# A decoder trunk on eight cores: convolution taps that read PSUM, SiLU on ScalarE, casts off GpSimd, and an instruction order planned with the contention of VectorE and GpSimd and with slack for TensorE

## The chip, the cores and the metric

The kernel runs on the 8 cores of one Trainium2 chip, each core with one prompt sequence of 2048 tokens and 16 sample sequences of 4 tokens. The metric is device time in microseconds (us) of the slowest core. These kernels have a second, slower state in some executions: the records of some cores show a lower TensorE clock than those of the others. Only fast runs are compared here.

Names: PE is TensorE (matmuls), PEld its weight loads, DVE is VectorE, ACT is ScalarE, POOL is GpSimd, SP is SyncE.

## The reference, cut to what matters

```python
def trunk_layer(x, c, h0, buf_a, buf_b, ...):          # four layers of this; cut
    shift, scale, gate = split(silu(c) @ w_c + b_c, 3)
    h = layer_norm(x) * (1 + scale) + shift
    a_x, a_z, b_cg, b_bg, b_x, b_z, g_a, g_b = split(h @ w_in)       # 8 x 1024 columns
    xa, new_buf_a = causal_conv(a_x, buf_a, conv_a_w)                # 4 taps
    xa = xa + conv_a_b
    hs, h_last = rglru(xa, ...)          # two block-diagonal gates of xa, exp, sqrt, a scan
    o_a = (hs * silu(a_z)) @ w_a_out
    yb, new_buf_b = causal_conv(b_cg * b_x, buf_b, conv_b_w)         # 3 taps
    o_b = (b_bg * yb * silu(b_z)) @ w_b_out
    out = (sigmoid(g_a) * o_a + sigmoid(g_b) * o_b) @ w_o
    res = ALPHA * x + gate * out
    return layer_norm(res) * ln_g + ln_b, ...
```

## The kernel before

Channels lie on the 128 partitions, tokens on the free axis. The 2112 tokens of a core are three jobs of W = 704, and a slot is one job in one layer. A projection for 128 channels of a job is 16 matmuls of 352 columns into a "pair", a PSUM tensor that the program declares as 128x1024 fp32, with 352 columns in use in each half of 512. The program has four pairs. A pair can be filled again only when every reader of its block is through.

The order of every engine's instructions is computed when the kernel is built. Operations are recorded with what they read and write, a modelled cost, and an engine. A greedy planner then simulates the five queues, takes for each engine the earliest candidate in a window, and assigns PSUM pairs. Its order is what runs; on the chip, semaphores enforce the dependencies. The loop of the planner in the kernel before:

```python
        while left:
            best = None
            for e in ENGS:
                lst = pend[e]
                if not lst:
                    continue
                window = PE_WINDOW if e == "pe" else EW_WINDOW
                cands = []
                for i, op in enumerate(lst[:window]):
                    rdy = 0.0
                    for d in op.deps:
                        if d.finish is None:
                            break
                        t = d.finish if d.eng == e and d.dma is None else d.finish + SYNC
                        if t > rdy:
                            rdy = t
                    else:
                        pr = None
                        if op.blk is not None and op.blk.pair is None:
                            pt = None
                            for k, users in enumerate(pairs):
                                t = 0.0
                                for u in users:
                                    if u.finish is None:
                                        break
                                    t = max(t, u.finish + SYNC)
                                else:
                                    if pt is None or t < pt:
                                        pt, pr = t, k
                            if pr is None:
                                continue
                            rdy = max(rdy, pt)
                        sw = e == "act" and op.tbl != 0 and op.tbl & cur_tbl == 0
                        st = max(rdy, free[e])
                        cands.append((st + (TBL_COST if sw else 0.0), i, op, sw, pr, st))
                if not cands:
                    continue
                first = min(c[0] for c in cands)
                c = min((c for c in cands if c[0] <= first + QUANT), key=lambda c: c[1])
                if best is None or c[0] < best[1][0]:
                    best = (e, c)
            assert best is not None, "no operation can be scheduled"
            e, (st, i, op, sw, pr, _) = best
            if e == "act" and op.tbl:
                cur_tbl = op.tbl if sw or cur_tbl == 0 else op.tbl & cur_tbl
            if pr is not None:
                have = set(map(id, op.deps))
                op.deps += [u for u in pairs[pr] if id(u) not in have]
                op.blk.pair = pr
                pairs[pr] = op.blk.users
            free[e] = st + op.cost
            if op.dma is not None:
                dma_free = max(dma_free, st + 1.0) + op.nbytes / DMA_RATE
                op.finish = dma_free + 1.2
            else:
                op.finish = st + op.cost + op.lat
            del pend[e][i]
            newq[e].append(op)
            left -= 1
        self.q = newq
        return max(free.values())
```

The modelled costs: a DVE operation of n columns is `0.1 + n * 1.04 / 1000` us (0.83 for 704), with 0.06 more for a scalar read per partition; a POOL operation is `0.2 + n * 0.0021` (1.68 for 704).

The operations that the change touches, for one chunk of 128 channels (c) of a slot. `act` goes to ACT, `tt` to the engine named, `stt` to DVE, `T(s)` is a slot of the SBUF tile TMP, `ps(blk)` the PSUM block:

```python
            def f_ax(c=c, x=x):
                x["u0"] = U.get()
                blk = Blk()
                proj(x["u0"], 0, blk)
                a = take("p1")
                r = x["xa"] = take("p1")
                pB = PSTB[l][c][1]
                cp("pool", T(a, 0, 3), PST[:, l, c, 1:4], [pB], [TMPB[a]])
                act(halves(T(r)), ps(blk), AF.Identity, [blk, PRMB], [TMPB[r]], bias=prm(l, c, 4), scale=prm(l, c, 3),
                    psum=True)
                act(halves(T(a, 3, 3 + W)), ps(blk), AF.Copy, [blk], [TMPB[a]], psum=True)
                cp("pool", PST[:, l, c, 1:4], T(a, npr, npr + 3), [TMPB[a]], [pB])
                if smp:
                    sv = v3(AXS[:, :], 7)
                    st = v3(SST[:, c, 16:64], 3)
                    cp("pool", sv[:, :, 0:3], st, [SSTB[c]], [AXSB], n=48)
                    cp("pool", sv[:, :, 3:7], v3(T(a, 3 + npr, 3 + W), ST), [TMPB[a]], [AXSB], n=64)
                    cp("pool", st, sv[:, :, 4:7], [AXSB], [SSTB[c]], n=48)
                for kk in (2, 1, 0):
                    stt(T(r, 0, npr), T(a, kk, kk + npr), prm(l, c, kk), T(r, 0, npr), ALU.mult, ALU.add,
                        [TMPB[a], PRMB, TMPB[r]], [TMPB[r]], n=npr)
                if smp:
                    xv = v3(T(r, npr, W), ST)
                    for kk in (2, 1, 0):
                        stt(xv, sv[:, :, kk:kk + ST], prm(l, c, kk), xv, ALU.mult, ALU.add,
                            [AXSB, PRMB, TMPB[r]], [TMPB[r]], n=NSMP)
                give("p1", a)
                b = x["xab"] = (k * NCH + c) % 2
                cp("pool", XAb[:, b, :], T(r), [TMPB[r]], [XAbB[b]], n=W)

            def f_az(c=c, x=x):
                blk = Blk()
                proj(x["u0"], 1, blk)
                U.release(x["u0"])
                z = x["tz"] = take("p1")
                act(halves(T(z)), ps(blk), AF.Tanh, [blk], [TMPB[z]], scale=0.5, psum=True)
                stt(halves(T(z)), halves(T(z)), 1.0, ps(blk), ALU.add, ALU.mult, [TMPB[z], blk], [TMPB[z]])
```

SiLU of a_z (and, alike, of b_z) is (tanh(z/2) + 1) * z: an ACT operation and a DVE operation that both read the pair. The short convolution and the gates, cut before their sample-token parts:

```python
            def f_cg(c=c, x=x):
                blk = Blk()
                proj(x["u1"], 0, blk)
                U.release(x["u1"])
                b = x["cb"]
                tt("dve", halves(T(b, 2, 2 + W)), ps(blk), halves(T(b, 2, 2 + W)), ALU.mult, [blk, TMPB[b]], [TMPB[b]])
                cp("pool", PST[:, l, c, 4:6], T(b, npr, npr + 2), [TMPB[b]], [PSTB[l][c][2]])
                y = x["yb"] = take("p1")
                act(T(y), T(b, 2, 2 + W), AF.Identity, [TMPB[b], PRMB], [TMPB[y]], scale=prm(l, c, 10))
                for kk in (1, 0):
                    stt(T(y, 0, npr), T(b, kk, kk + npr), prm(l, c, 8 + kk), T(y, 0, npr), ALU.mult, ALU.add,
                        [TMPB[b], PRMB, TMPB[y]], [TMPB[y]], n=npr)
            ...
            def f_gate(c=c, x=x):
                b, xa = x["xab"], x["xa"]
                br, bi = Blk(), Blk()
                for o, blk in ((0, br), (1, bi)):
                    mm(blk, [(wcol(WG, c, o), lambda t, b=b: XAb[:, b, t * HW:(t + 1) * HW])], [WGB, XAbB[b]])
                r, i, m = take("p1"), take("p1"), take("p1")
                act(halves(T(r)), ps(br), AF.Tanh, [br, DERB], [TMPB[r]], bias=HB[:, 0, l, c:c + 1], scale=0.5, psum=True)
                act(halves(T(i)), ps(bi), AF.Tanh, [bi, DERB], [TMPB[i]], bias=HB[:, 1, l, c:c + 1], scale=0.5, psum=True)
                s = SH[:, l, c:c + 1]
                act(T(r), T(r), AF.Exp, [TMPB[r], DERB], [TMPB[r]], bias=s, scale=s)
                act(T(m), T(r), AF.Square, [TMPB[r]], [TMPB[m]])
                stt(T(i), T(i), 1.0, T(xa), ALU.add, ALU.mult, [TMPB[i], TMPB[xa]], [TMPB[i]])
                act(T(m), T(m), AF.Sqrt, [TMPB[m]], [TMPB[m]], bias=0.25, scale=-0.25)
                tt("pool", T(i), T(i), T(m), ALU.mult, [TMPB[i], TMPB[m]], [TMPB[i]])
                hB = PSTB[l][c][0]
                ...
```

## Time and profile before

| kernel before | value |
|---|---|
| time, median of 3 runs | 2960.91 us (2958.0 to 2961.5) |
| undisturbed core 5 of the profiled run: span, clock | 2955.3 us, 0.976 |
| PE / DVE / ACT / POOL busy on core 5 | 2690 / 2236 / 1648 / 1490 us |
| PE waits on core 5, all together | 242 us |

The profiled execution: cores 2 and 3 took 3005.5 and 3005.9 us at a clock of 0.952, the other six 2953 to 2956 us at 0.975 to 0.977. Every reading below is therefore of core 5, which is undisturbed.

From core 5's page, the busy line (time, share of the span, instructions) and the chain that ended last, by engine and then by line of the kernel:

```profile
PE 2690.3 (91%) x18144; PEld 1735.5 (59%) x18144; DVE 2235.9 (76%) x2521; ACT 1648.1 (56%) x1967; POOL 1490.3 (50%) x1818
...
PE 68%; DVE 14%; issue 10%; ACT 5%; POOL 1%; DMA 1%; DVEq 0%; SPq 0%; ACTq 0%; POOLq 0%
PE PS L398 67%; DVE TMP L378 6%; DVE TMP L374 6%; ACT TMP L365 4%; DMA X<-x 1%; ACT L365 1%; DVE X L378 1%; DVE TMP L579 1%; POOL TMP L374 1%; ACT X L365 1%; PE PS L773 0%; DVEq L209 0%; DVE X L374 0%; DVE MG L374 0%; ACT HN L365 0%
```

PE is busy for 91% of the span and makes up 68% of the chain. The other 32% of the chain is work of other engines that PE waited for, and time in which an engine waited for nothing that the profile shows (issue).

Busy times by stretch of the span, same core. The columns after the length are busy time and count of instructions by engine, then the granted clock, the DMA share and GB/s:

```profile
core 5: us, PE busy (x) PEld busy (x) DVE busy (x) ACT busy (x) POOL busy (x), PEclk, DMA share, GB/s
0.00:215.00 215.00, 124.08 (x947) 78.14 (x948) 150.20 (x161) 114.36 (x144) 109.13 (x124) 0.94 0.85 153
215.00:2600.00 2385.00, 2252.47 (x15155) 1455.57 (x15154) 1850.54 (x2056) 1376.86 (x1638) 1239.82 (x1501) 0.98 0.76 131
```

The first 215 us are the start-up. After that, between 215 and 2600 us, PE is idle for 2385 - 2252.5 = 132.5 us. In stretches without a stall, 136 to 137 matmuls start in 20 us, 146.5 ns each.

What PE waited for on that core (the releaser; us in total, times, longest):

```profile
engine line waited for: us in total, times, longest us
PE PS L398 <- DVE TMP L378: 91.7, 56, 3.6
PE PS L398 <- DVE LNR L374: 47.4, 5, 31.0
PE PS L398 <- ACT TMP L365: 40.3, 26, 5.0
PE PS L398 <- DVE TMP L374: 15.1, 19, 1.5
```

The four largest are shown; the whole list adds up to 242 us. The largest releaser is the DVE scalar_tensor_tensor on TMP. SiLU and the merge end with such an operation as the last reader of their block, so a pair stays taken until DVE gets to it. The wait for LNR is mostly the start (31.0 us at once).

Groups of instructions kept apart by shape, core 5 (busy us, mean ns of one; then idle time before them and what ended it):

```profile
L378 DVE SCALAR_TENSOR_TENSOR TMP<-TMP,PRM 128x704 f32<-128x704 f32 x320 | 368.2, 1151 | 133.4 <-ACT TMP L365 111.7 <-DVE TMP L378 1.8
L378 DVE SCALAR_TENSOR_TENSOR TMP<-TMP,PS 128x704 f32<-128x704 f32 x384 | 335.1, 879 | 130.4 <-PE PS L398 102.7 <-ACT TMP L365 26.2
...
L365 ACT ACT_TABLE_LOAD x227 | 291.2, 1283 | 49.6 <-PE PS L398 44.8 <-DVE TMP L378 1.3
...
L374 DVE TENSOR_TENSOR TMP<-X,TMP 128x704 f32<-128x704 f32 x192 | 208.3, 1089 | 11.1 <-ACT TMP L365 7.9 <-ACT HN L365 1.4 <-ACT X L365 0.7
...
L378 DVE SCALAR_TENSOR_TENSOR X<-PS,MOD,X 128x704 f32<-128x704 f32 x64 | 60.3, 943 | 28.5 <-PE PS L398 28.5
```

The first group holds convolution taps (two SBUF inputs), the second SiLU and the merge (one PSUM input). They have the same shape and the same operation, but take 1.151 and 0.879 us. The timeline shows where the difference comes from (x2 is two operations shown as one; of the taps, the window that was asked for cuts off a third):

```profile
start us, us, engine line op out<-in xcount [idle before <-releaser]
...
1416.26 1.68 POOL L374 TENSOR_TENSOR YB<-TMP 128x704 bf16<-128x704 f32 x1 [4.08 <-DVE TMP L374]
...
1416.82 4.14 DVE L374 TENSOR_TENSOR TMP<-X,TMP 128x704 f32<-128x704 f32 x2
1417.89 2.32 POOL L374 TENSOR_TENSOR TMP<-TMP 128x704 f32<-128x704 f32 x1
...
1422.83 3.50 DVE L378 SCALAR_TENSOR_TENSOR TMP<-TMP,PRM 128x704 f32<-128x704 f32 x2
...
1423.90 1.68 POOL L374 TENSOR_TENSOR YA<-TMP 128x704 bf16<-128x704 f32 x1
```

Two DVE operations (x2) that need about 0.9 us each take 4.14 us beside two POOL multiplies, and of the two taps (3.50 us together) the one beside another multiply takes 2.46 us; one of the three POOL multiplies takes 2.32 us, the others 1.68.

Sorted one by one in core 5's trace, the 184 taps of 704 columns that had no POOL operation beside them (DMA issues not counted) took 0.950 us in the mean and at most 0.954; the 105 that had one beside them for over half of their time took 1.559 us. SiLU and merge, with their PSUM input, took 0.883 us without POOL and 0.875 beside it. So a tap from SBUF is slower only where POOL runs.

### The profile page before, as it was taken

How to read it: one execution, taken by the hardware profiler on the slowest of the kernel's cores; microseconds unless marked ns; L12 is line 12 of the kernel's file. 1: busy time of each engine (PE TensorE's matmuls, PEld its weight loads, DVE VectorE, ACT ScalarE, POOL GpSimd, SP SyncE). 2: the span in 40 equal slices, each digit the busy share in tenths (PEclk: the TensorE clock that was granted, in tenths of full speed). 3: DMA queues.
4: the chain of work that ended last, by engine and by line, in shares of the span. 5: the costliest groups of instructions: out<-in, count | busy, mean ns of one | idle time of the engine just before them, and what ended most of it. 6: DMA issues, size and time to landing. Idle time of an engine off the chain costs nothing.

```text
span 3005.9 us, 54078 instructions; the slowest of 8 cores (2953.4 to 3005.9 us)
## 1 busy us (share of the span) xinstructions
PE 2753.6 (92%) x18144; PEld 1758.7 (59%) x18144; DVE 2243.5 (75%) x2521; ACT 1648.4 (55%) x1967; POOL 1487.4 (49%) x1818
## 2 busy tenths in 40 slices
PE   1789998999999999999999999899999899999996
PEld 1456665665565666565565566566556566566553
DVE  3886678778668778878877877877866787776745
ACT  3665556546546556555564655654645655653532
POOL 3574356455336436546535535655543653644611
PEclk9899999998899999999999999999889999999977
DMA  9878987877787887786897797777767578687671
GB/s 189 150 115 126 148 119 123 147 106 143 116 135 107 154 154 107 134 146 100 149 157 116 140 156 122 138 131 109 137 98 134 88 132 152 103 170 117 94 164 50
DMA packets 116479, 389.03 MB, mean 129 GB/s; under 512 B 12912, under 2 KB 13168, under 8 KB 116208
## 3 DMA queue, kind: packets, MB, share of 16 engines
q0 software_dynamic: 83520, 304.12, 67.2%
q1 hardware_dynamic: 32688, 81.45, 8.7%
q8 instruction: 151, 2.47, 0.3%
q14 instruction: 120, 0.98, 0.1%
HBM read 653.33 MB, written 36.27 MB: 229 GB/s over the span
## 4 chain that ended last, share of the span: by engine, by line
PE 72%; DVE 12%; issue 8%; ACT 5%; POOL 1%; DMA 1%; DVEq 0%; SPq 0%; ACTq 0%; POOLq 0%
PE PS L398 72%; DVE TMP L378 5%; DVE TMP L374 5%; ACT TMP L365 3%; DMA X<-x 1%; ACT L365 1%; DVE X L378 1%; POOL TMP L374 1%; DVE TMP L579 1%; ACT X L365 0%; PE PS L773 0%; DVEq L209 0%; POOL PST L389 0%; ACT HN L365 0%; POOL SST L389 0%
## 5 line engine op out<-in xcount | busy, mean ns | idle before, releaser
L398 PE MATMUL PS<-HN,WB 128*128 128x352 bf16 x12288 | 1983.6, 322 | 131.3 <-DVE TMP L378 73.0
L398 PEld LDWEIGHTS PS<-HN,WB 128*128 128x128 bf16 x12288 | 1224.4, 100 | 833.9 <-issue 156.8
L365 ACT ACTIVATE TMP<-PS 128x704 f32<-128x704 f32 x624 | 461.0, 752 | 420.0 <-PE PS L398 381.4
L378 DVE SCALAR_TENSOR_TENSOR TMP<-TMP,PRM 128x704 f32<-128x704 f32 (+1 forms) x480 | 524.7, 1093 | 184.1 <-ACT TMP L365 151.4
L404 POOL DMA_DIRECT2D WB<-wmain x528 | 295.4, 560 | 619.8 <-PE PS L398 506.3
L374 POOL TENSOR_TENSOR TMP<-TMP 128x704 f32<-128x704 f32 x240 | 435.0, 1814 | 166.1 <-ACT TMP L365 157.5
L378 DVE SCALAR_TENSOR_TENSOR TMP<-TMP,PS 128x704 f32<-128x704 f32 x384 | 335.2, 880 | 158.9 <-PE PS L398 123.0
L365 ACT ACTIVATE TMP<-X 128x704 f32<-128x704 f32 x192 | 149.5, 788 | 335.4 <-DVE X L378 146.3
L365 ACT ACT_TABLE_LOAD x227 | 291.2, 1283 | 56.3 <-PE PS L398 51.7
L389 POOL COPY PST<-TMP 128x1 f32<-128x1 f32 (+2 forms) x288 | 146.6, 509 | 285.5 <-ACT TMP L365 146.7
L398 PE MATMUL PS<-YB,WB 128*128 128x352 bf16 x1536 | 255.0, 321 | 8.5 <-DVE TMP L378 8.5
L398 PE MATMUL PS<-YA,WB 128*128 128x352 bf16 x1536 | 255.0, 321 | 0.1
L374 POOL TENSOR_TENSOR YB<-TMP 128x704 bf16<-128x704 f32 x96 | 180.2, 1878 | 143.1 <-DVE TMP L374 139.1
L398 PE MATMUL PS<-MG,WB 128*128 128x352 bf16 x1536 | 245.4, 317 | 5.0 <-DVE TMP L378 2.8
L374 DVE TENSOR_TENSOR TMP<-PS,TMP 128x704 f32<-128x704 f32 x192 | 170.1, 886 | 97.2 <-PE PS L398 93.4
L374 DVE TENSOR_TENSOR TMP<-X,TMP 128x704 f32<-128x704 f32 x192 | 208.7, 1091 | 14.3 <-ACT TMP L365 11.1
L365 ACT ACTIVATE TMP<-TMP,PRM 128x704 f32<-128x704 f32 x96 | 84.6, 881 | 240.6 <-DVE TMP L374 238.2
L398 PEld LDWEIGHTS PS<-YB,WB 128*128 128x128 bf16 x1536 | 152.9, 100 | 94.8 <-issue 10.6
L374 DVE TENSOR_TENSOR TMP<-TMP 128x704 f32<-128x704 f32 x192 | 181.5, 950 | 31.4 <-ACT TMP L365 21.3
L398 PEld LDWEIGHTS PS<-MG,WB 128*128 128x128 bf16 x1536 | 151.8, 99 | 88.4 <-issue 6.7
L398 PEld LDWEIGHTS PS<-YA,WB 128*128 128x128 bf16 x1536 | 153.2, 100 | 85.4 <-issue 0.8
L365 ACT ACTIVATE TMP<-TMP 128x704 f32<-128x704 f32 (+1 forms) x241 | 190.1, 789 | 20.9 <-DVE TMP L579 3.6
(56 smaller groups left out, 2100.8 us busy)
## 6 DMA issues: line engine op xcount, KB each, us to landing
WB<-wmain POOLq DMA_DIRECT2D x528, 512.0 KB, 7.5
xres<-X SPq DMA_DIRECT2D x72, 352.0 KB, 11.1
X<-xres SPq DMA_DIRECT2D x72, 352.0 KB, 8.5
WB<-wc POOLq DMA_DIRECT2D x48, 512.0 KB, 8.7
X<-x SPq DMA_DIRECT2D x48, 352.0 KB, 9.8
y<-X SPq DMA_DIRECT2D x24, 352.0 KB, 5.9
WG<-wmain POOLq DMA_DIRECT2D x4, 512.0 KB, 7.2
SST<-sst SPq DMA_DIRECT2D x4, 384.0 KB, 7.8
```

The lines of the kernel that those rows point to most:

```text
L365: return P.add("act", lambda e: e.activation(out=res(out), in_=res(in_), func=func, **kw), reads, writes, cost=0.14 + 0.09 * nap + n * 0.0 ...
L374: return P.add(eng, lambda e: e.tensor_tensor(out=res(out), in0=res(in0), in1=res(in1), op=op), reads, writes, cost=cost, lat=0.05)
L378: return P.add("dve", lambda e: e.scalar_tensor_tensor(out=res(out), in0=res(in0), scalar=scalar, in1=res(in1), op0=op0, op1=op1), reads, ...
L389: return P.add(eng, lambda e: e.tensor_copy(out=res(out), in_=res(in_)), reads, writes, cost=(0.19 + n * 0.0009) if eng == "pool" else dco ...
L398: ins = e.matmul(PS[blk.pair][:, t * 512:t * 512 + HW], w, mov(t), start=(i == 0), stop=(i == len(steps) - 1))
L404: return P.add(eng, lambda e: e.dma_start(out=out, in_=src), reads, writes, dma=tag, cost=0.56 if eng == "pool" else 0.08, nbytes=nbytes)
L579: P.add("dve", lambda e: e.tensor_tensor_scan(out=T(m), data0=T(r), data1=T(i), initial=PST[:, l, c, 0:1], op0=ALU.mult, op1=ALU.add), [TM ...
```

## The change

Its intent: give DVE less to do and less contention, free PSUM sooner, and make the planned order hold on the chip. The parts:

1. Matmul outputs of a pair become contiguous (the first 352 columns move to the end of the first half of 512), so that one access of 704 columns runs over both halves, with 160 free columns in front. Taps read the pair itself, at an offset; the 2 or 3 columns of history are copied in front of it.
2. SiLU is one ACT operation.
3. Casts and history copies move from POOL to ACT.
4. The planner plans POOL's operations and those of DVE without a PSUM operand one after another, as if they shared one thing (the field `port`; "the port" below is this part of the plan, a model of the stretch from 0.950 to 1.559 us above); DVE costs get 0.05 us more; PE prefers blocks that have been ready for 2 us in the plan.
5. All accesses to a block are put in one chain, each depending on the last. It was put in for correctness; every kernel here orders these accesses, so no run shows whether it is needed.

The diff, cut to its core (the cuts are marked with ...):

```diff
-TSL = 708
+TSL = 704
+P0 = 512 - HW
+PE_SLACK = 2.0
...
+        for b in list(reads) + list(writes):
+            if isinstance(b, Blk) and b.users:
+                deps[id(b.users[-1])] = b.users[-1]
...
                         st = max(rdy, free[e])
-                        cands.append((st + (TBL_COST if sw else 0.0), i, op, sw, pr, st))
+                        if op.port:
+                            st = max(st, port_free)
+                        key = max(rdy + PE_SLACK, st) if pe else st + (TBL_COST if sw else 0.0)
+                        cands.append((key, i, op, sw, pr, st + (TBL_COST if sw else 0.0)))
...
             free[e] = st + op.cost
+            if op.port:
+                port_free = st + op.cost
...
-    def dcost(n, k=1.04, o=0.1):
+    def dcost(n, k=1.04, o=0.15):
...   # tt, stt: port=not psum; scan: port=True; POOL copies: port=True
-                    ins = e.matmul(PS[blk.pair][:, t * 512:t * 512 + HW], w, mov(t), start=(i == 0),
+                    ins = e.matmul(PS[blk.pair][:, P0 + t * HW:P0 + (t + 1) * HW], w, mov(t), start=(i == 0),
...   # f_ax
-                cp("pool", T(a, 0, 3), PST[:, l, c, 1:4], [pB], [TMPB[a]])
-                act(halves(T(a, 3, 3 + W)), ps(blk), AF.Copy, [blk], [TMPB[a]], psum=True)
-                cp("pool", PST[:, l, c, 1:4], T(a, npr, npr + 3), [TMPB[a]], [pB])
+                act(lambda: pv(-3, 0), PST[:, l, c, 1:4], AF.Copy, [blk, pB], [hist], n=3)
+                act(PST[:, l, c, 1:4], lambda: pv(npr - 3, npr), AF.Copy, [blk], [pB], n=3)
...
-                    stt(T(r, 0, npr), T(a, kk, kk + npr), prm(l, c, kk), T(r, 0, npr), ALU.mult, ALU.add,
-                        [TMPB[a], PRMB, TMPB[r]], [TMPB[r]], n=npr)
+                    stt(T(r, 0, npr), lambda kk=kk: pv(kk - 3, kk - 3 + npr), prm(l, c, kk), T(r, 0, npr), ALU.mult,
+                        ALU.add, [blk, hist, PRMB, TMPB[r]], [TMPB[r]], n=npr, psum=True)
...
-                cp("pool", XAb[:, b, :], T(r), [TMPB[r]], [XAbB[b]], n=W)
+                act(XAb[:, b, :], T(r), AF.Copy, [TMPB[r]], [XAbB[b]])
...   # f_az, f_bz
-                act(halves(T(z)), ps(blk), AF.Tanh, [blk], [TMPB[z]], scale=0.5, psum=True)
-                stt(halves(T(z)), halves(T(z)), 1.0, ps(blk), ALU.add, ALU.mult, [TMPB[z], blk], [TMPB[z]])
+                act(T(z), ps(blk), AF.Silu, [blk], [TMPB[z]], psum=True)
...   # f_cg: the product C*x is written back into PSUM, and its taps read it there
-                tt("dve", halves(T(b, 2, 2 + W)), ps(blk), halves(T(b, 2, 2 + W)), ALU.mult, [blk, TMPB[b]], [TMPB[b]])
+                tt("dve", pv, pv, T(b), ALU.mult, [blk, TMPB[b]], [blk], psum=True)
...   # f_gate is split in two (f_gr, f_gi), one block each; factors of 2 of the old SiLU go
```

## The prediction

> **What bounds it now.** TensorE. On an undisturbed core (core 5, 2955.3 us) the page shows PE busy 2690 us (91%), DVE 2236 (76%), ACT 1648 (56%), POOL 1490 (50%); the chain that ended last is 68% PE, 14% DVE, 5% ACT. In windows without a stall PE runs 136 to 137 matmuls of 352 columns in 20 us, 146.5 ns each: 2530 us for the 17280 main ones, some 2580 with the rest. So 375 us are loss:
> - Start and end, about 150 us: first projection near 67 us, a 41 us wait for LayerNorm sums, a drain after 2925 us. Not touched.
> - PE waits in the middle (215 to 2750 us): about 130 of the 242 us that the list of waits gives PE. The largest releaser is DVE's scalar_tensor_tensor on TMP (92 us in all), then ACT on TMP (40), DVE tensor_tensor (15): mostly PSUM pairs not yet free, where DVE is busy 16 to 19 us of 20.
> - Half clock: the clock records show some 25 stretches of 3.4 to 10 us at 0.5 after such gaps, 116 us before the final drain; about 40 us of loss in the middle.
>
> About 170 us is within reach.
>
> **What the change does** (means from the groups kept apart by shape).
> - DVE: 192 (t+1)*z operations of SiLU go (x 0.879 = 169 us). 480 convolution taps read PSUM instead of SBUF: 1.151 us falls to about 0.88 (the same operation with a PSUM input), together -110 us. [...]GpSimd contends with DVE instructions that have two SBUF inputs; the trace agrees: those average 0.95 to 1.34 us and pass 2 us while POOL runs, those with a PSUM input stay at 0.88. DVE about 1920 us.
> - POOL: casts (90), history and state copies (200) go: about 1200 us.
> - ACT: gains 96 casts (76 us) and some 450 tiny PSUM copies of about 0.2 (95), loses 96 copies (72). SiLU adds a third table set per chunk: loads from 227 to about 300 at 1.283 us, +95. About 1840 us.
> - PSUM: the a_x and C*x blocks are held through a serial ACT/DVE chain, 4 to 5 us after their matmuls instead of 1 to 2; SiLU blocks are freed after one ACT instruction instead of two operations. Four pairs at 2.35 us each tolerate about 7 us, so this costs little on average.
> - PE order: blocks ready for 2 us in the plan are preferred, so small errors of the plan no longer stop PE.
>
> **Critical path.** DVE and POOL savings count only where PE waits for PSUM: of 170 us I expect 100 back (70 of waits, 30 of clock).
>
> **Predicted: 2857 us** (-3.5%), range 2790 to 2930. Chances: faster by over 2% 0.77, within 2% 0.19, slower 0.04.
>
> **What would show it.** PE idle in 215 to 2750 falls to about 60 us; PE busy about 2655; granted clock from 0.976 to about 0.985; taps near 0.88; DVE, POOL and ACT as above, about 300 table loads; start and end unchanged. PE's remaining waits name ACT and taps, no longer SiLU operations.
>
> **What would make it wrong.** Too many table switches, so ACT frees PSUM late and PE waits move from DVE to ACT (2900 or more); serial PSUM chains holding pairs past 7 us[...]. If the planned slack removes nearly all gaps, 2790.

## The result, and the profile after

The kernel after is correct. Its five executions took 2798.25, 2798.84 and 2799.12 us in the fast state and 2958.95 and 3044.74 us in the slow one (the profiled execution is one of the fast). The comparison is of the fast runs: ratio 0.9454, 95% interval 0.9436 to 0.9473, so 5.5% faster. Ratios here are the mean time of one kernel's fast runs over that of the other's of the same rounds, so not quite the ratio of the medians. In the two slow runs the cores of die 0 show clocks of 0.894 to 0.934 and spans of 2934 to 3043 us, while die 1 stays at 2789 to 2797 us.

Core 5 of the kernel after, the busy line and the chain that ended last:

```profile
PE 2646.1 (95%) x18144; PEld 1728.7 (62%) x18144; DVE 1940.9 (69%) x2297; ACT 1818.5 (65%) x2482; POOL 1153.9 (41%) x1274
...
PE 85%; ACT 7%; DVE 4%; issue 3%; DMA 1%; POOL 0%; SPq 0%; ACTq 0%; DVEq 0%; POOLq 0%
PE PS L401 84%; ACT TMP L368 4%; DVE TMP L381 2%; ACT L368 2%; DMA X<-x 1%; DVE TMP L377 1%; PE PS L771 0%; DVE PS L377 0%; ACT PST L368 0%; ACT XAb L368 0%; ACT PS L368 0%; POOL YA L377 0%; SPq L407 0%; POOL TMP L377 0%; ACTq L224 0%
```

Its busy times by the same stretches:

```profile
core 5: us, PE busy (x) PEld busy (x) DVE busy (x) ACT busy (x) POOL busy (x), PEclk, DMA share, GB/s
0.00:215.00 215.00, 135.15 (x1070) 87.54 (x1071) 137.55 (x159) 139.59 (x195) 93.69 (x100) 0.95 0.89 162
215.00:2600.00 2385.00, 2348.36 (x16014) 1536.19 (x16012) 1679.14 (x1978) 1588.17 (x2168) 1002.23 (x1108) 1.00 0.77 139
```

Its PE waits:

```profile
engine line waited for: us in total, times, longest us
PE PS L401 <- ACT TMP L368: 45.4, 36, 7.5
PE PS L401 <- DVE LNR L377: 35.0, 2, 28.8
PE PS L771 <- DMA WB<-wc: 15.6, 2, 11.0
```

Its groups by shape, answering to those shown of before:

```profile
L368 ACT ACT_TABLE_LOAD x294 | 377.2, 1283 | 56.1 <-PE PS L401 47.7 <-DVE TMP L381 1.3
L381 DVE SCALAR_TENSOR_TENSOR TMP<-PS,PRM,TMP 128x704 f32<-128x704 f32 x320 | 303.1, 947 | 142.7 <-ACT PST L368 70.7 <-ACT TMP L368 51.4 <-PE PS L401 3.4
...
L377 DVE TENSOR_TENSOR TMP<-X,TMP 128x704 f32<-128x704 f32 x192 | 176.6, 922 | 50.7 <-ACT TMP L368 44.2 <-ACT HN L368 2.7 <-ACT X L368 1.5
...
L381 DVE SCALAR_TENSOR_TENSOR TMP<-TMP,PS 128x704 f32<-128x704 f32 x192 | 169.1, 883 | 176.2 <-PE PS L401 175.5
...
L381 DVE SCALAR_TENSOR_TENSOR X<-PS,MOD,X 128x704 f32<-128x704 f32 x64 | 60.4, 944 | 21.0 <-PE PS L401 20.3
```

The span of core 5 falls by 2955.3 - 2796.4 = 158.9 us. PE's waits fall from 242 to 128 us in all, which is 114. PE's busy time falls by 44.2 us for the same 18144 matmuls. Most of this is half clock: the clock records list 24 stretches of it, 116.1 us, before the final drain in the kernel before, and 9 stretches, 44.4 us, after. In them PE was busy for 98.4 and 34.6 us; half of the difference, 32 us, is an estimate of what half clock cost (the other 12 us are not explained). (They last 3.4, 6.8 or 10.2 us. Of the 3.4 us before each of them PE was idle for 1.8 us or more. In them matmuls of 352 columns start 293 ns apart in the median, in both kernels, against the 146.5 ns of stretches without a stall: hence half.) The two terms make 158 of the 158.9 us. Between 215 and 2600 us PE is now idle for 36.6 us, from 132.5. The first projection begins at 67.1 us in both, and the longest wait for LNR is 31.0 and 28.8 us, but PE's idle time in the first 215 us falls from 91 to 80 us. The end is the same: the last projection's last matmul starts about 30 us before the end in both.

That tells where the time came from, but not which part of the change brought it. DVE has 295 us less to do, and the order is another one as well.

### The profile page after: what moved, and what is told of

Read it like the earlier page. It is cut to its first block, busy times and chain, and to the rows that moved or that the text cites. A ratio compares the mean times of both kernels' runs of the same rounds, so it can differ in the third digit from the quotient of the medians.

```text
span 2796.7 us, 53655 instructions; the slowest of 8 cores (2789.3 to 2796.7 us)
## 1 busy us (share of the span) xinstructions
PE 2646.0 (95%) x18144; PEld 1728.5 (62%) x18144; DVE 1940.9 (69%) x2297; ACT 1818.4 (65%) x2482; POOL 1153.8 (41%) x1274
## 4 chain that ended last, share of the span: by engine, by line
PE 85%; ACT 6%; DVE 4%; issue 3%; DMA 1%; POOL 0%; SPq 0%; ACTq 0%; DVEq 0%; POOLq 0%
PE PS L401 85%; ACT TMP L368 4%; DVE TMP L381 2%; ACT L368 2%; DMA X<-x 1%; DVE TMP L377 1%; PE PS L771 0%; DVE PS L377 0%; ACT XAb L368 0%; POOL YA L377 0%; ACT PST L368 0%; ACT PS L368 0%; SPq L407 0%; POOL TMP L377 0%; ACTq L224 0%
## 5 line engine op out<-in xcount | busy, mean ns | idle before, releaser
L401 PE MATMUL PS<-HN,WB 128*128 128x352 bf16 x12288 | 1913.8, 314 | 51.0 <-ACT TMP L368 31.9
L401 PEld LDWEIGHTS PS<-HN,WB 128*128 128x128 bf16 x12288 | 1201.1, 98 | 698.0 <-issue 64.4
L368 ACT ACTIVATE TMP<-PS 128x704 f32<-128x704 f32 x528 | 392.8, 754 | 298.1 <-PE PS L401 284.9
L381 DVE SCALAR_TENSOR_TENSOR TMP<-PS,PRM,TMP 128x704 f32<-128x704 f32 (+1 forms) x480 | 443.8, 924 | 192.0 <-ACT TMP L368 73.3
L381 DVE SCALAR_TENSOR_TENSOR TMP<-TMP,PS 128x704 f32<-128x704 f32 x192 | 169.1, 883 | 176.3 <-PE PS L401 175.5
L401 PE MATMUL PS<-YA,WB 128*128 128x352 bf16 x1536 | 244.6, 312 | 1.5 <-DVE TMP L381 1.5
L377 DVE TENSOR_TENSOR TMP<-X,TMP 128x704 f32<-128x704 f32 x192 | 176.6, 922 | 50.8 <-ACT TMP L368 44.2
L368 ACT ACTIVATE TMP<-PS,PRM 128x704 f32<-128x704 f32 x192 | 170.8, 889 | 43.9 <-PE PS L401 33.0
L381 DVE SCALAR_TENSOR_TENSOR TMP<-TMP 128x704 f32<-128x704 f32 (+1 forms) x97 | 129.1, 1331 | 84.5 <-ACT TMP L368 70.5
L583 DVE TENSOR_TENSOR_SCAN TMP<-TMP,PST 128x704 f32<-128x704 f32 x96 | 163.9, 1707 | 30.1 <-POOL TMP L377 18.4
```

Source lines behind the costliest of these rows:

```text
L368: return P.add("act", lambda e: e.activation(out=res(out), in_=res(in_), func=func, **kw), reads, writes, cost=0.14 + 0.09 * nap + n * 0.0 ...
L377: return P.add(eng, lambda e: e.tensor_tensor(out=res(out), in0=res(in0), in1=res(in1), op=op), reads, writes, cost=cost, lat=0.05, port=n ...
L381: return P.add("dve", lambda e: e.scalar_tensor_tensor(out=res(out), in0=res(in0), scalar=scalar, in1=res(in1), op0=op0, op1=op1), reads, ...
L401: ins = e.matmul(PS[blk.pair][:, P0 + t * HW:P0 + (t + 1) * HW], w, mov(t), start=(i == 0), stop=(i == len(steps) - 1))
L583: P.add("dve", lambda e: e.tensor_tensor_scan(out=T(m), data0=T(r), data1=T(i), initial=PST[:, l, c, 0:1], op0=ALU.mult, op1=ALU.add), [TM ...
```

## The experiments

All times are medians of fast runs, and all ratios are against fast runs of the kernel before, taken on the same chip in the same rounds. The fast runs of before lie between 2955 and 2972 us on all chips, but for one of 2990. What a part is worth is worked out as the difference of two ratios times 2960 us; the kernel after, at 0.9454, gains 162 us by that measure. Every kernel gave a correct result.

At first there were two theories. R (relief, the prediction's): fewer and shorter DVE and POOL operations free PSUM sooner. P (the plan): the new order is what counts.

### u_plan: new operations, old planner

```diff
-                        if op.port:
-                            st = max(st, port_free)
-                        key = max(rdy + PE_SLACK, st) if pe else st + (TBL_COST if sw else 0.0)
+                        key = st + (TBL_COST if sw else 0.0)
...   # DVE offsets 0.15 and 0.21 back to 0.1 and 0.16
```

> The kernel after, ordered by the planner of before (no slack for TensorE, no shared port, the old DVE costs); operations, engines and PSUM use stay. Theory R (relief: fewer and shorter DVE and GpSimd operations free the PSUM pairs sooner, order is secondary) expects about 2820 us, at most a quarter of the 160 us given back, ratio to before about 0.955. Rival P (the plan: order with slack is what removed PE's waits) expects 2880 us or more, ratio 0.972 to 1.0, with PE's waits back above 190 us.

Measured: 2900.2 us, ratio 0.980 (0.9784 to 0.9816). The new operations alone are worth 59 us, not 162. PE's waits on core 5 are 204 us, from 128 in the kernel after. R misses by 80 us; P holds.

```profile
engine line waited for: us in total, times, longest us
PE PS L399 <- ACT TMP L366: 55.5, 46, 2.9
PE PS L399 <- DVE TMP L379: 42.2, 26, 3.6
PE PS L399 <- DVE LNR L375: 37.7, 3, 30.6
```

### b_plan: old operations, new planner

The converse: the planner's part of the diff applied to the kernel before, with the port marked on DVE operations that have no PSUM operand, on the scan, and on POOL operations.

> The kernel before, ordered by the new planner (slack 2 us for TensorE, shared port of DVE and GpSimd, new DVE costs); its operations stay. R expects 2930 us or more (ratio 0.99 to 1.0), since DVE keeps its 2236 us of work and PE still waits for PSUM pairs that it holds. P expects 2860 us or less (ratio at most 0.967).

Measured: fast runs at 2851.0, 2854.5 and 2854.7 us; ratio 0.9645 (0.9623 to 0.9668). The plan alone is worth 105 us, with the old operations; P holds again. PE's waits fall from 242 to 166 us, while DVE and POOL keep nearly all their work, as core 5's busy line shows:

```profile
PE 2658.8 (93%) x18144; PEld 1731.7 (61%) x18144; DVE 2190.5 (77%) x2521; ACT 1649.6 (58%) x1967; POOL 1437.1 (50%) x1818
```

DVE is 45 us below the 2235.9 us of before, for the same operations. So the order took away a little of the contention, but mostly it placed DVE's work where PE doesn't wait for it:

```profile
engine line waited for: us in total, times, longest us
PE PS L407 <- ACT TMP L373: 43.8, 28, 4.7
PE PS L407 <- DVE TMP L386: 42.4, 29, 2.5
PE PS L407 <- DVE LNR L382: 34.9, 2, 28.9
```

### u_silu and u_taps: the operations one by one

u_silu puts Tanh and the DVE multiply back, in the new plan (with them the factors of 2, and the planner's table set for Tanh, as in the kernel before):

```diff
-                act(T(z), ps(blk), AF.Silu, [blk], [TMPB[z]], psum=True)
+                act(T(z), ps(blk), AF.Tanh, [blk], [TMPB[z]], scale=0.5, psum=True)
+                stt(T(z), T(z), 1.0, ps(blk), ALU.add, ALU.mult, [TMPB[z], blk], [TMPB[z]], psum=True)
```

> The kernel after, with SiLU as before: Tanh on ACT, then (t+1)*z on DVE from PSUM, 192 of them. DVE gains about 170 us, ACT loses some 65 table loads (85 us), and the a_z and b_z blocks hold their PSUM pair about 1.5 us longer. R expects about 2840 us (ratio 0.96): a quarter of the gain. P expects within 10 us of the kernel after (2800).

Measured: 2817.4 us, ratio 0.9519 (0.9504 to 0.9534). SiLU on ACT is worth 19 us, between the two forecasts. DVE is busy 2065 us, 125 more than in the kernel after.

u_taps puts the convolution inputs back into SBUF (history copies stay on ACT):

```diff
+                act(T(a, 3, 3 + W), pv, AF.Copy, [blk], [TMPB[a]], psum=True)
...
-                    stt(T(r, 0, npr), lambda kk=kk: pv(kk - 3, kk - 3 + npr), prm(l, c, kk), T(r, 0, npr), ALU.mult,
-                        ALU.add, [blk, hist, PRMB, TMPB[r]], [TMPB[r]], n=npr, psum=True)
+                    stt(T(r, 0, npr), T(a, kk, kk + npr), prm(l, c, kk), T(r, 0, npr), ALU.mult,
+                        ALU.add, [TMPB[a], PRMB, TMPB[r]], [TMPB[r]], n=npr)
...   # likewise for C*x
```

> The kernel after, with the convolution inputs evacuated to SBUF by ACT (or written there by DVE) and the 480 taps read from SBUF, history copies still on ACT. DVE gains at least 60 us through slower taps, ACT gains 72 us of evacuation; the a_x and C*x pairs are held for two operations instead of a chain of six. R expects about 2830 us (ratio 0.957). P expects within 10 us of 2800. If the serial chain on a PSUM pair costs more than the taps gain, it is faster than the kernel after.

Measured: 2838.1 us, ratio 0.959 (0.9575 to 0.9605). DVE is busy 2095 us, 154 more than in the kernel after. Taps from PSUM are worth 40 us, close to R's forecast and not to P's: relief counts too, only for less than the plan. And the longer serial chain on a PSUM pair costs less than the taps gain.

### u_cast: the casts back on GpSimd

```diff
-                act(XAb[:, b, :], T(r), AF.Copy, [TMPB[r]], [XAbB[b]])
+                cp("pool", XAb[:, b, :], T(r), [TMPB[r]], [XAbB[b]], n=W)
```

> The kernel after with the 96 casts of the gate input back on GpSimd (about 0.94 us each there, 0.79 on ACT). ACT falls by 76 us to 1743, GpSimd rises to about 1240. If ACT, now PE's main releaser (45 us of waits), is what is short, this is faster by 5 to 15 us; if the cast off GpSimd helped as the change meant it to, slower by 5 to 20 us.

Measured: 2797.4 us, ratio 0.945 (0.9434 to 0.9466). The difference from the kernel after is about 1 us, which is nothing. Neither expectation holds; taken by itself, this part is worth nothing. The three parts of the operations sum to 19 + 40 - 1 = 58 us. That agrees with the 57 us between b_plan and the kernel after, and with the 59 us of u_plan: the operations' gains add up, and are about the same under both planners. How exact that is, is not shown: each run is one order, and a changed order alone can move the time by 10 us or more (see "What the plan says of itself").

### u_slack, s4 and u_port: the parts of the planner

These three and u_cast ran on one chip. The second question was which part of the planner works: S (slack) or C (truer costs of DVE and POOL).

u_slack sets `PE_SLACK = 0.0`:

> The kernel after with the planner's slack for TensorE set from 2.0 us to 0; shared port and new DVE costs stay in the plan. The old planner as a whole gave 2900 us against 2799. Theory S (the slack is the working part: PE takes blocks whose inputs and PSUM pair were ready long before) expects at least two thirds of that back: 2870 us or more (ratio 0.97). Rival C (the plan got better because its DVE and GpSimd costs got truer) expects 2830 us or less (ratio 0.957).

Measured: 2799.3 us, ratio 0.9456 (0.9438 to 0.9475): no difference from the kernel after. With these operations the slack is worth nothing, and S falls.

s4 sets `PE_SLACK = 4.0`:

> The kernel after with the slack doubled, 4.0 us. If plan error is what still stops PE (waits of 60 us after 215 us), S expects 2785 to 2795 us (ratio 0.942). If 2 us already covers it, no change within 5 us; if the longer slack makes PE pass over blocks that the other engines need, slower.

Measured: 2811.2 us, ratio 0.9497 (0.948 to 0.9513): about 12 us slower. The plan itself is then 11 us longer (2788 us against 2777).

u_port leaves the port out of the plan:

```diff
-                        if op.port:
-                            st = max(st, port_free)
```

> The kernel after with the shared port of DVE and GpSimd left out of the plan (both may be planned at the same time); slack and costs stay. S expects within 15 us of the kernel after (2799 us, ratio 0.945 to 0.95), since slack covers errors of the plan; C expects 2840 us or more (ratio 0.96).

Measured: 2889.9 us, ratio 0.9765 (0.9745 to 0.9784). These two lines are worth 92 us of the 162. C holds. No operation, engine or cost differs from the kernel after, only the order and the PSUM pairs that the planner hands out with it. PE's waits are 197 us:

```profile
engine line waited for: us in total, times, longest us
PE PS L399 <- ACT TMP L366: 67.2, 51, 4.5
PE PS L399 <- DVE LNR L375: 37.5, 3, 30.5
PE PS L399 <- DVE TMP L379: 21.1, 21, 3.0
```

Core 5's busy line for that run:

```profile
PE 2665.1 (92%) x18144; PEld 1730.1 (60%) x18144; DVE 1992.8 (69%) x2297; ACT 1812.8 (63%) x2479; POOL 1170.5 (41%) x1274
```

DVE is 52 us above the kernel after and POOL 17, so the order of the kernel after avoids some of the stretch. In both kernels the engines' work fits the span; the difference lies in PE's waits (197 against 128 us) and busy time (2665 against 2646). Without the port, slack and truer DVE costs together are worth about 10 us here (u_port against u_plan); the costs alone were not tried.

### b_noport and b_s0: the same on the old operations

b_noport is b_plan without the two lines of the port; b_s0 is b_plan with slack 0. (The port alone, with old costs and no slack, could not be built: the greedy planner ran into a dead end.)

A new theory, X, speaks of operations that "exclude one another". So the plan treats them; in the traces they overlap and get longer, as the taps did beside POOL: 1.559 us against 0.950.

> The kernel before, ordered by the new planner with slack 2 us and the new DVE costs, but without the shared port. With the port the same operations gave 2853 us. Theory X (the plan must know which DVE and GpSimd operations exclude one another) expects 2920 us or more here, ratio 0.985 or more, and the chip over 130 us behind the plan's own 2780 us. Its rival for the old operations (slack or costs did it) expects 2870 us or less, ratio 0.97.

Measured: median 2922.6 us, ratio 0.9885 (0.9848 to 0.9923). Without the port the plan is worth 34 us with the old operations; with it 105. The port is again the larger part, 71 us, as X expected.

> The kernel before, ordered with the shared port and the new DVE costs, slack 0. The plan's own estimate is 2819 us (2793 with slack 2). X expects 2860 to 2890 us, ratio 0.966 to 0.976: most of the gain with the port alone, the chip some 60 us behind the plan as with slack 2. If slack is what pays on these operations, 2920 us or more, ratio 0.986.

Measured: 2887.2 us, ratio 0.9757 (0.9724 to 0.9789), inside X's range, at its upper end. But slack is then worth 33 us with the old operations, where it was worth nothing with the new ones (26 of the 33 are in the plan's own length, as shown below). "Slack does nothing" would be wrong as a general statement.

### u_flat: is it the mean load, or the exclusion?

The port is left out, but the mean stretch is charged flat to each operation. The 0.22 us is an estimate from u_port's groups: its DVE operations with two SBUF inputs of 704 columns took 0.994 to 1.353 us by groups of 96 or more, in the mean 1.10, against 0.88 in the plan.

```diff
-        cost = 0.2 + n * 0.0021 if eng == "pool" else dcost(n)
+        cost = 0.33 + n * 0.0021 if eng == "pool" else dcost(n) + (0.0 if psum else 0.22)
...   # the same 0.22 in stt, scan 0.2 to 0.37; and without the two lines of the port
```

> The kernel after without the shared port in the plan, but with the mean stretch that the traces show charged flat: 0.22 us more for each DVE operation with two SBUF inputs, 0.17 for a scan, 0.13 for a GpSimd operation; slack stays. X expects it near the kernel without port, 2860 us or more, ratio 0.966: the mean is right, but not which operation is late. Rival L (the plan only had too little load) expects 2830 us or less, ratio 0.956.

Measured: 2823.1 us, ratio 0.9537 (0.9511 to 0.9564). Theory X misses by 37 us, and L's range holds. Of the 92 us that the port brings, charging the mean brings 67, and planning the operations one after another brings the other 25. Only this one flat charge was tried.

### What the plan says of itself

When the kernel is built, the planner prints the length of its own plan. This is an estimate by the kernel's program, not a measurement, but how far the chip falls behind it is telling:

| kernel | contention in the plan | plan's estimate | chip, fast | behind |
|---|---|---|---|---|
| before | none | 2775 | 2961 | 186 |
| u_plan | none | 2751 | 2900 | 149 |
| b_noport | none | 2780 | 2923 | 143 |
| u_port | none | 2794 | 2890 | 96 |
| b_s0 | port | 2819 | 2887 | 68 |
| b_plan | port | 2793 | 2855 | 62 |
| u_flat | mean, flat | 2775 | 2823 | 48 |
| u_taps | port | 2805 | 2838 | 33 |
| u_slack | port | 2769 | 2799 | 30 |
| u_silu | port | 2788 | 2817 | 29 |
| u_cast | port | 2774 | 2797 | 23 |
| s4 | port | 2788 | 2811 | 23 |
| after | port | 2777 | 2799 | 22 |
| best (below) | port | 2753 | 2772 | 19 |

The kernels before and after have nearly the same plan, 2775 and 2777 us. What changed is that the chip now nearly keeps to it. The old plan ignored a delay that the trace shows (1.559 us for a tap beside POOL, where the plan has 0.89), so its queues were ordered for times that never came true; each engine works through its queue in the planned order, and so the delay could reach PE.

The table also tells a difference in the plan's length from one in the chip's keeping to it. The port's gain is of the second kind: with it the chip falls behind by 22 us instead of 96 (new operations) and 62 instead of 143 (old ones), while the plan's length changes by only -17 and +13. So a plan that merely came out shorter is no rival here. The same holds for the last step from u_flat (2775, 48 behind) to after (2777, 22 behind). But where the port is in both plans, the difference is mostly in the plan's length: 28 of the 40 us of the taps, 11 of the 19 of SiLU, 11 of the 12 of s4, 26 of the 33 of slack with the old operations. The planner is greedy, and its length moves by 3 to 26 us when a setting changes. A gain of that size, like SiLU's 19 us, can be the order's and not the operation's; these runs don't separate the two.

### best: both neutral parts taken the other way

Since the plan could now be believed, it was used to choose: of about 100 settings tried in the planner alone (some of which it could not finish), casts on GpSimd with slack 0 had one of the shortest plans, 2753 us.

```diff
-PE_SLACK = 2.0
+PE_SLACK = 0.0
...
-                act(XAb[:, b, :], T(r), AF.Copy, [TMPB[r]], [XAbB[b]])
+                cp("pool", XAb[:, b, :], T(r), [TMPB[r]], [XAbB[b]], n=W)
```

> The kernel after with two things that cost nothing or gained each: the casts back on GpSimd and slack 0. The plan's own estimate falls from 2777 to 2753 us, and the chip was 22 to 33 us behind the plan wherever the port was in it, so 2775 to 2790 us is expected, ratio 0.937 to 0.943.

Measured: fast runs at 2770.2 to 2772.6 us, ratio 0.9365 (0.9339 to 0.9391). It is 6.3% faster than the kernel before, and 26 us faster than the kernel after (by ratios that are from different rounds and chips). The chip is 19 us behind the plan, and 24 of the 26 us stand in the plan's length: the two parts, of which neither gained anything alone, gave a shorter order together. (The "22 to 33 us behind" of the expectation is true of the new operations only; b_plan and b_s0 were 62 and 68 behind.) PE's waits on core 5 are 110 us, and the largest releaser among them, with 35 us, is the LNR of the start.

## Why the prediction was right or wrong

Right:
- The bound: PE, with loss split over start and end (untouched), waits in the middle, and half clock after the waits. PE's waits (114 us) and PE's busy time (44 us, about 32 of them half clock) give the whole gain. Of PE's idle time, 91 us went between 215 and 2750 us (from 133.8 to 42.4, forecast about 60), 11 in the start, which was to stay as it was. The granted clock of core 5 is 0.987 (forecast 0.985).
- The time: 2799 us in fast runs lies in the range of 2790 to 2930, and faster by over 2% had 0.77.
- The engines' new loads. Predicted and measured: DVE 1920 and 1941 us, POOL 1200 and 1154, ACT 1840 and 1818, PE 2655 and 2646; about 300 table loads, and 294. The 1.283 us of a table load was the same in both traces.
- PE's remaining waits name ACT, no longer SiLU operations on DVE. (Taps were to be named too; all DVE TMP operations of their line hold PE for 6.8 us only.)

Wrong in size: "of 170 us I expect 100 back (70 of waits, 30 of clock)". The chip gave back 159: 114 of waits and 44 of busy time, of which the clock, by the estimate above, is about 32. So the clock term was about right, and the waits were forecast too small. What that forecast lacked is the plan. That 2799 us lies in the range is partly luck: its lower end, 2790, was given for the case that "the planned slack removes nearly all gaps". The gaps went, but with these operations the slack had no part in it.

- The prediction wrote of the planner only "PE order: blocks ready for 2 us in the plan are preferred, so small errors of the plan no longer stop PE". It took the slack for the working part. With these operations and the port in the plan the slack is worth nothing (u_slack); with the old ones 33 us (b_s0). The port, which the prediction didn't count in the plan at all, is worth 92 and 71 us.
- The prediction saw the contention itself (0.88 against 0.95 to 1.34 us, over 2 us beside POOL) but booked it as DVE time to be saved. Its larger cost was that the plan didn't know of it: 92 us of span between u_port and the kernel after, with 52 us of DVE time. The sign was there to be read: the costs stand in the code, 0.83 us for a DVE operation of 704 columns, and the trace has 0.95 to 1.34 for those with two SBUF inputs.
- "DVE and POOL savings count only where PE waits for PSUM" was right here: the new operations brought 57 to 59 us for 250 to 266 us less DVE time (b_plan to the kernel after, before to u_plan).

Wrong in a cost: "1.151 us falls to about 0.88 (the same operation with a PSUM input), together -110 us". Taps of 704 columns take 0.947 us from PSUM. They read their weight from a [128,1] operand, and the operation chosen for comparison has an immediate. The right one stood in the same view: X<-PS,MOD,X with such an operand took 0.943 us before. The taps' saving is 521.4 - 443.8 = 78 us, by the groups of both. A tap of 704 columns without POOL beside it took 0.950 us from SBUF, so reading PSUM made it no faster in itself: all that it saved is the stretch beside POOL.

What brings the slow state isn't shown: the kernel after (PE 95% busy) ran slow in 2 of 5 executions, u_slack (95%) in none of 4, and the kernel before (91%) in 4 of 11 on one chip.

Left open: why the greedy planner's order of the old operations is 26 us longer without slack, and that of the new ones 8 us shorter; and whether the chain of accesses to a PSUM pair costs anything by itself, since no kernel without it was tried.

## What to carry to other kernels

When an order is computed from modelled costs, compare the plan's length with the chip's first: a gap (186 us of 2961 here) is time that a truer model may bring back. Compare the model's cost of each operation with its mean in the trace, kept apart by shape and by where its inputs lie; where the two differ, look for what the model leaves out: here it was another engine. When two kernels differ by little, see first whether their plans differ by as much. And a saving on an engine that is not the bound is worth only the waits that it ends: here 250 to 266 us less DVE time brought 57 to 59 us, and two lines in the planner 92.

## What else the traces show

- DVE operations of 704 columns with two SBUF inputs averaged 0.95 to 1.34 us in the kernel before, against 0.88 to 0.95 where no POOL operation ran beside them, and two of them took 4.14 us beside two POOL operations. Two orders of the same operations, with and without the port in the plan, differ by 92 us of span, though by only 52 us of DVE time and 17 of POOL.
- A scalar_tensor_tensor of 704 columns with one PSUM input took 0.943 us with a scalar read from a [128,1] operand and 0.879 with an immediate, 0.06 us less.
- The planner takes Tanh to share one table set with SiLU and another with Exp. By that its order has 295 loads; with Tanh and Exp alone sharing a set the same order would need 521, counted in the plan. 295 ran on core 5 (the 294 above and one at the start), and the results were correct.
- In the profiled execution of before, the clock records of cores 2 and 3 list some 450 us at 0.8125 each (mean clock 0.952), while those of cores 0 and 1 of the same die list none (0.975 and 0.976).
